# Where the weights of narrow matmuls stand in SBUF: 192 bytes into their buffers, other tiles at equal addresses

## The chip, the cores and the metric

The kernel runs on one core of one Trainium2 chip. The metric is the device time of one execution in microseconds (us). A time "of the runs" is the median of timed executions; a profile is one more execution, with its own time.

## The reference

Two layers of a diffusion backbone over 256 context tokens and 256 latent tokens of 1024 features, in float32. A layer is half a SwiGLU FFN, a token mixer (layer 0: bidirectional mLSTM; layer 1: bidirectional retention), and half an FFN; each of these six sub-layers is normed and modulated by a linear map of the condition. The last FFN runs for the latent tokens alone.

```python
def half_ffn(h, mod, g, w13, w2, j):
    return h + FFN_RES * mod[:, :, 3 * j + 2] * swiglu(modnorm(h, g, mod, j), w13, w2)
def swiglu(h, w13, w2):
    a, b = jnp.split(h @ w13, 2, axis=-1)
    return (jax.nn.silu(a) * b) @ w2
for i in range(DEPTH):
    ...
    x = half_ffn(x, mod_x, norm_g[i, 0], ffn_w13[i, 0], ffn_w2[i, 0], 0)
    ctx = half_ffn(ctx, mod_c, norm_g[i, 0], ffn_w13[i, 0], ffn_w2[i, 0], 0)
    ...
return rmsnorm(x, final_g)
```

D_MODEL is 1024, D_FF 2816.

## The kernel before

**Units.** All weights come as units of 1 MB (some of 512 KB), one DMA each from SP's queue, three units ahead, into one of three `raw` buffers. `split(n, half)` turns each half of a unit (128x1024 numbers) into a high part `wh` (ACT, L147) and a low part `wl` (DVE, L148), each in one of four buffers. TensorE (PE) then makes three products of a tile pair for each 128x128 block of weights: `mm3` (L151 to L153) multiplies high by high, high by low and low by high into the same PSUM bank. Activations are split in the same way: `xh`, `xl` (the normed stream, 512 tokens wide: 256 context, 256 latent), `gh`, `gl` (the middle of an FFN), `yh`, `yl` (the middle of retention), and `qh`, `kh`, `vh`, `Ph` with their low parts.

**Widths.** A product's moving operand has 512 columns where both segments go together, and 256 where one goes alone. The four FFNs are named by layer and place: FFN(0,0), FFN(0,1), FFN(1,0), FFN(1,1). In the first three the w2 products are 240 matmuls of 512 columns in the first of two parts, and 192 of 512 and 192 of 256 in the second: the last two units of the second part run segment by segment, so that the norm of the context segment can be made under the products of the latent one. FFN(1,1) has 22 w13 units and 11 w2 units of 48 matmuls each, all of 256 columns. Of 256 columns are also: the first two w13 units of FFN(0,1) and FFN(1,0) (192 matmuls each), the mLSTM's `qk(0)` (96) and its last two output units (192), retention's `proj_k(0)` (96), its four `proj_q` (192), its scores (96) and its eight output units with `yh`, `yl` (384).

**Addresses.** PE loads the weights of the next matmul (LDWEIGHTS) while the moving operand of the present one streams. Both are read from SBUF. In the built program `xh`, `xl`, `wh` and `wl` all start 224 bytes past a multiple of 256, and every block in them starts a multiple of 512 bytes further on. So moving and stationary operands of these products stand at **equal addresses**, as this document calls it: their distance is a multiple of 256 bytes. For `gh` and `gl` the kernel takes `shift` numbers of a filler tile `gf` ahead of them, so they stand 0 bytes (FFN(0,0)), 32 (FFN(0,1)), 64 (FFN(1,0)) and 128 (FFN(1,1)) past the weights' place. `yh` and `yl` come to stand 96 past it; retention's own products (scores, values) have equal addresses. Both ways of standing, which operand is moving and which stationary, occur: `Y<-xh,wh` may have `xh` as the stationary one.

**Order.** A scheduler orders the instructions of each engine; the first stage's order is written out by hand. The first DMAs on SP's queue are `VT` (all vectors), then `XT` (the stream); POOL's queue brings `ident` and `cst` (the two triangular masks `up` and `low`, used at L643 and L644 in the mLSTM's gates).

Of the kernel before, what the change touches and what calls it, by code (L numbers as in the profile page):

```python
# [87 lines left out]
def build(nc, tc, dr, out):  # L88
# [32 lines left out]

    V.memset(fill.tile([128, 24], F32, name="fill"), 0.0)
    ident = const.tile([128, 128], F32, name="ident")
    nc.gpsimd.dma_start(out=ident, in_=dr["c1"][:, 0:128])
    cst = const.tile([128, 258], F32, name="cst")
    nc.gpsimd.dma_start(out=cst, in_=dr["c1"][:, 128:386])
    up, low = cst[:, 0:128], cst[:, 128:256]
# [4 lines left out]
    VT = const.tile([128, 256], F32, name="VT")  # L132
    XT = const.tile([128, KT, NT], F32, name="XT")
# [7 lines left out]
    FG = VT[:, 64:72]  # L141
    CW = VT[:, 72:112]
    MB = VT[:, 112:256]

# [130 lines left out]
    def ffn(l, which, segs, groups, on_tile, on_seg, first="seg"):  # L275
# [3 lines left out]
        st = ExitStack()  # L279
        shift = (0, 8, 16, 32)[2 * l + which]  # L280
        P = {}
# [5 lines left out]
        def start(W):  # L287
            if groups:
                mp["r"] = pool("mr", 3, st)
                if first == "k":  # L290
                    mp["c"], mp["j"] = U["mc"], U["mj"]
                else:
                    mp["c"] = mc = pool("mc", 1, st).tile([128, 2, DM], F32, name="mc")
                    mp["j"] = pool("mj", 1, st).tile([128, DM], mybir.dt.bfloat16, name="mj")
                    nc.gpsimd.dma_start(out=mc.rearrange("p w k -> p (w k)"), in_=dr["cc"].to_broadcast([128, 2 * DM]))
                    for w in range(2):
                        S.activation(out=mc[:, w], in_=mc[:, w], func=AF.Silu)
            if shift:
                G.memset(pool("gf", 1, st).tile([128, shift], F32, name="gf"), 0.0)
            P["g"] = pool("g", 12, st)  # L300
            P["s"] = pool("s", 4, st)
# [3 lines left out]
        for d0, nd in parts:  # L305
            for p in range(d0, d0 + nd, 2):
                sv = {}
                for ab in range(2):
# [41 lines left out]
                    if first == "k" and p == 0:  # L350
                        def fn0(W, ab=ab, sv=sv):
                            sv["ps", ab] = U["ps", ab] = {m: bankA() for m in range(2)}
                            first_products[ab](W)
                        res.append((fn0, src, "own"))
                        late.append((lambda W, done=done: done(), None, None))
                        if ab:
                            res += [(start, None, None)] + late
                    else:
                        res.append((fn, src, "k"))
            ku = [(k, min(4, d0 + nd - k)) for k in range(d0, d0 + nd, 4)]  # L360
            fin = d0 == parts[-1][0]
            for mg in range(2):
                Y = {}
                for k0, nk in ku:
# [100 lines left out]
    def mlstm(on_tile, on_seg):  # L465
# [26 lines left out]
        def qk(u):  # L492
            src = win[:, u * 256:(u + 1) * 256].rearrange("(k p) c -> p k c", p=128)

            def fn(W):
# [10 lines left out]
                for m in range(2):  # L506
# [11 lines left out]
                    S.activation(out=X["q" if c < 4 else "k"][:, c % 4, :], in_=cv, func=AF.Silu)  # L518
            return (fn, src, "k")

# [35 lines left out]
        def wout(hh, u):  # L556
# [30 lines left out]
            def fn1(W):  # L587
# [7 lines left out]
                on_seg(1)  # L595
            return ((fn, src, "k") if hh == 0 else (fn0, src, "k") if u == 0 else (fn1, src, "k2"))

# [22 lines left out]
    def gates(X):  # L620
# [21 lines left out]
        ps = gb[:, 128:256]  # L642
        TE.matmul(ps[:, 0:32], up, lf[:, 0:32], start=True, stop=True)  # L643
        TE.matmul(ps[:, 32:64], low, lf[:, 32:64], start=True, stop=True)  # L644
        TE.matmul(ps[0:1, 64:128], ones[:, 0:1], lf, start=True, stop=True)
# [196 lines left out]
    def retention(on_tile, on_seg):  # L842
# [5 lines left out]
        def start(W):  # L848
# [6 lines left out]
            X["cos"], X["sin"] = tb[:, 1536:1792], tb[:, 1792:2048]  # L855
            dec = p.tile([128, 8], F32, name="dec")
            nc.sync.dma_start(out=dec, in_=dr["r_dec"].to_broadcast([128, 8]))
            lg = p.tile([128, 8], F32, name="lg")
            logsig(lg, dec, 8)
            nl = p.tile([128, 8], F32, name="nl")  # L860
            V.tensor_scalar(out=nl[:, 0:4], in0=lg[:, 0:4], scalar1=-128.0, scalar2=None, op0=ALU.mult)
# [21 lines left out]
        def proj_k(h):  # L883
            X[h] = H = {}

            def fn(W):
# [13 lines left out]
                rope([z[:, :, 256:512] for z in H["k"]], pp[0][:, 256:512], pp[1][:, 256:512])  # L900
            return (fn, win[:, 1024 + h * 256:1024 + (h + 1) * 256].rearrange("(k p) c -> p k c", p=128), "eo")

        def proj_q(h):
            H = X[h]

            def fn(W):
                H["q"] = pair("q", [128, 2, 256])
                pp = [bankA() for _ in range(2)]
                for hf in range(2):
                    for e in range(2):  # L910
                        for k in range(hf * 4, hf * 4 + 4):
                            mm3(pp[e][:, 0:256], [W(i, k)[:, e, :] for i in range(2)],
                                (xh[:, k, 256:512], xl[:, k, 256:512]), k == 0, k == KT - 1)
# [3 lines left out]
            return (fn, win[:, h * 256:(h + 1) * 256].rearrange("(k p) c -> p k c", p=128), "eo")  # L917

# [107 lines left out]
        def outp(h):  # L1026
            r = []
            for u in range(2):
                src = dr["r_out"][h * 512:(h + 1) * 512, u * 512:(u + 1) * 512].rearrange("(k p) c -> p k c", p=128)

                def fn(W, u=u):
# [13 lines left out]
                    if h == 3 and u == 1:  # L1045
                        on_seg(1)
                r.append((fn, src, "k"))
            return r
# [73 lines left out]
    def first_stage():  # L1122
# [144 lines left out]
    def split(n, half):  # L1267
# [8 lines left out]
        if mode == "eo":  # L1276
            src_ = src_.rearrange("p (a c e) -> p a e c", a=na, e=2)
# [32 lines left out]
    for i, (fn, src, mode) in enumerate(steps):  # L1310
# [11 lines left out]
        with ExitStack() as late:  # L1322
            if n == 2:
                for z in ("hi", "lo"):
                    late.enter_context(tc.issue_after(U[z, 5].ins))
            split_to(2 * n + (2 if mode == "k2" else 3))
        fn(Unit(n, src))
# [1 line left out]
```

## Time and profile before

| | us |
|---|---|
| median of 3 runs (1915.36 to 1919.32) | 1918.21 |
| profiled execution, its own time | 1913.94 |
| its span, first to last instruction | 1912.1 |

The span is what the rows further down divide up. PE is busy in nearly all of it; its clock was granted at 0.991 of full speed on average.

### The profile page before, as it was taken

What the parts mean: (1) busy time and instruction counts of PE and PEld (TensorE: products, weight loads), DVE (VectorE), ACT (ScalarE), POOL (GpSimd) and SP (SyncE); (2) the same over time, 40 slices, a digit from 0 to 9 for tenths busy, and PEclk for the clock granted to TensorE, in tenths of its full rate; (3) what the DMA queues carried; (4) which work ended last, traced back from release to release, by engine and by line L of the source; (5) the groups of instructions that cost most, each with busy time, mean ns of one, the idle gap of its engine ahead of it and who ended that gap; (6) DMA issues with size and microseconds to landing.
All of it is one profiled execution on the core that took longest, in us unless ns stands there. A gap on an engine that the chain in (4) does not pass through costs nothing.

```text
span 1912.1 us, 25440 instructions
## 1 busy us (share of the span) xinstructions
PE 1878.6 (98%) x10142; PEld 1617.0 (85%) x10142; DVE 1192.0 (62%) x1965; ACT 696.8 (36%) x1061; POOL 167.2 (9%) x207
## 2 busy tenths in 40 slices
PE   8999999999999999999999999999999999999998
PEld 6888888887777898888888988888898888889998
DVE  6858878566866566677764655555466555565554
ACT  4432232243553352222333422223244444444443
POOL 3000000110132210000001000000112120110001
PEclk9999999999998999999999999999999999989999
DMA  8536656223323234455542344554334244235652
GB/s 315 194 125 209 209 176 206 91 86 99 102 94 100 100 100 139 148 198 176 187 176 89 111 145 167 187 195 165 116 105 129 98 138 132 99 123 170 205 177 89
DMA packets 171689, 280.58 MB, mean 147 GB/s; under 512 B 6210, under 2 KB 108738, under 8 KB 171186
## 3 DMA queue, kind: packets, MB, share of 16 engines
q1 hardware_dynamic: 168656, 268.59, 42.0%
q0 software_dynamic: 2912, 10.36, 1.7%
q8 instruction: 80, 1.31, 0.3%
q14 instruction: 39, 0.31, 0.0%
q10 hardware_dynamic: 2, 0.01, 0.0%
HBM read 277.82 MB, written 1.11 MB: 146 GB/s over the span
## 4 chain that ended last, share of the span: by engine, by line
PE 91%; DVE 4%; ACT 2%; DMA 1%; issue 1%; POOL 1%; SPq 0%; POOLq 0%; DVEq 0%; ACTq 0%
PE A L152 18%; PE A L151 18%; PE A L153 18%; PE Y L152 11%; PE Y L151 11%; PE Y L153 11%; PE A L794 1%; PE A L797 1%; PE Y L1095 1%; DVE wl L148 1%; DMA XT<-xt 0%; DMA t<-nwd 0%; ACT wh L147 0%; DVE XT L210 0%; DVE so L551 0%
## 5 line engine op out<-in xcount | busy, mean ns | idle before, releaser
L148 DVE TENSOR_TENSOR wl<-raw,wh 128x1024 fp32r<-128x1024 f32 x360 | 448.0, 1245 | 465.9 <-ACT wh L147 465.6
L147 ACT ACTIVATE wh<-raw 128x1024 fp32r<-128x1024 f32 x360 | 382.2, 1062 | 808.1 <-PE A L152 324.7
L152 PE MATMUL A<-xl,wh 128*128 128x512 f32 (+1 forms) x1712 | 599.5, 352 | 6.8 <-DVE xl L148 6.1
L153 PE MATMUL A<-xh,wl 128*128 128x512 f32 (+1 forms) x1712 | 598.2, 351 | 0.0
L151 PE MATMUL A<-xh,wh 128*128 128x512 f32 (+1 forms) x1712 | 592.4, 352 | 5.6 <-ACT xh L1112 2.6
L152 PEld LDWEIGHTS A<-xl,wh 128*128 128x128 f32 x1712 | 325.8, 190 | 51.0 <-DVE xl L148 7.6
L151 PEld LDWEIGHTS A<-xh,wh 128*128 128x128 f32 x1712 | 321.5, 191 | 48.9 <-ACT xh L1112 2.9
L153 PEld LDWEIGHTS A<-xh,wl 128*128 128x128 f32 x1712 | 325.8, 190 | 42.4
L247 DVE CUSTOM_DVE_ANT_0 mj<-mr,mc,VT 128x1024 bf16<-128x1024 f32 x224 | 287.0, 1281 | 4.7 <-DMA mr<-mod_t 1.9
L153 PE MATMUL Y<-gh,wl 128*128 128x512 f32 (+1 forms) x704 | 246.0, 350 | 0.0
L151 PE MATMUL Y<-gh,wh 128*128 128x512 f32 (+1 forms) x704 | 245.5, 350 | 0.0
L152 PE MATMUL Y<-gl,wh 128*128 128x512 f32 (+1 forms) x704 | 245.3, 349 | 0.0
L153 PEld LDWEIGHTS Y<-gh,wl 128*128 128x128 f32 x704 | 132.3, 188 | 18.5
L152 PEld LDWEIGHTS Y<-gl,wh 128*128 128x128 f32 x704 | 132.4, 188 | 18.2
L151 PEld LDWEIGHTS Y<-gh,wh 128*128 128x128 f32 x704 | 132.3, 188 | 17.5
L152 PE MATMUL Y<-wl,xh 128*128 128x512 f32 x320 | 126.2, 395 | 0.0
L151 PE MATMUL Y<-wh,xh 128*128 128x512 f32 x320 | 125.3, 393 | 0.0
L153 PE MATMUL Y<-wh,xl 128*128 128x512 f32 x320 | 125.0, 392 | 0.0
L173 POOL TENSOR_TENSOR nacc<-nacc,nsq 128x256 f32<-128x256 f32 x50 | 41.6, 840 | 644.8 <-ACT nsq L169 643.4
L147 ACT ACTIVATE gh<-s 128x512 fp32r<-128x512 f32 (+1 forms) x88 | 48.7, 568 | 84.9 <-DVE s L338 84.9
L210 DVE SCALAR_TENSOR_TENSOR XT<-Y,GT,XT 128x256 f32<-128x256 f32 x148 | 63.8, 477 | 21.3 <-PE Y L153 21.1
L338 DVE TENSOR_TENSOR s<-s,A 128x512 f32<-128x512 f32 (+1 forms) x88 | 54.3, 619 | 28.5 <-PE A L153 28.2
(269 smaller groups left out, 1826.2 us busy)
## 6 DMA issues: line engine op xcount, KB each, us to landing
raw<-w SPq DMA_DIRECT2D x126, 1024.0 KB, 5.2
mr<-mod_t SPq DMA_DIRECT2D x128, 512.0 KB, 3.9
raw<-r_in SPq DMA_DIRECT2D x24, 1024.0 KB, 5.2
raw<-m_in SPq DMA_DIRECT2D x12, 1024.0 KB, 5.3
raw<-r_out SPq DMA_DIRECT2D x8, 1024.0 KB, 5.6
raw<-w SPq DMA_DIRECT2D x12, 512.0 KB, 3.7
w<-mod_t SPq DMA_DIRECT2D x8, 512.0 KB, 10.7
w<-mod_s SPq DMA_DIRECT2D x8, 512.0 KB, 10.6
```

The lines of the kernel that those rows point to most:

```text
L147: S.activation(out=hi, in_=src, func=AF.Copy)
L148: return V.tensor_tensor(out=lo, in0=src, in1=hi.bitcast(F32), op=ALU.subtract)
L151: TE.matmul(ps, l[0], r[0], start=first, stop=False)
L152: TE.matmul(ps, l[0], r[1], start=False, stop=False)
L153: return TE.matmul(ps, l[1], r[0], start=False, stop=last)
L173: G.tensor_tensor(out=N[s][0], in0=N[s][0], in1=sq, op=ALU.add)
L210: V.scalar_tensor_tensor(out=XT[:, k, seg(s)], in0=ps, scalar=gate[:, s, k:k + 1], in1=XT[:, k, seg(s)], op0=ALU.mult, op1=ALU.add)
L247: V.tensor_tensor_reduce(out=mp["j"], in0=raw[i], in1=mp["c"][:, w], scale=1.0, scalar=MB[:, l * 72 + f:l * 72 + f + 1], op0=ALU.mult, op1 ...
L338: V.tensor_tensor(out=g[:, a:z], in0=sv[m][:, a:z], in1=ps[m][:, a:z], op=ALU.mult)
L794: TE.matmul(ps[:, i, :], E[:, i * 4 + g * 2 + c], v[:, s * 2 + c, 2 * i + g, :], start=True, stop=(n == 0))
L797: TE.matmul(ps[:, i, :], WI[o:o + 64, i, c * 128:c * 128 + 128], X["C", d, n - 1][o:o + 64, i], start=False, stop=True)
L1095: TE.matmul(ps, U["w", k][:, 0, c * 128:(c + 1) * 128], SC.rearrange("p (w k) -> p k w", w=2)[:, c], start=(c == 0), stop=(c == KT - 1))
```

## The change

Four things. **(1)** `wh` and `wl` become 64 numbers (256 bytes) longer, and a unit whose matmuls are 256 columns wide, marked by an `n` at the end of its mode, is written 48 numbers (192 bytes) into them. A unit with 512 columns starts at 0 as before. **(2)** The filler `gf` goes, so `gh` and `gl` stand at equal addresses with a buffer's start in all FFNs; a small `fill0` brings all these tiles to a multiple of 256 bytes. `yh` and `yl` get there too. Retention's `q` pair is placed 64 bytes into a longer tile. In the built program every product of 256 columns with weights, and every score, then has its moving operand 64 bytes past the stationary one (counted modulo 256, that is 192 before it), and every product of 512 columns with weights has equal addresses (but for the mLSTM's gate weights `b4`, 96 before and after). **(3)** `VT` is cut in two: 72 columns stay for good (288 bytes a partition), 184 (`VB`: conv weights and modulation biases, 736 bytes) go to a pool that is closed ahead of retention. **(4)** The masks leave `cst` and are loaded at the mLSTM's start into a buffer of tag `hs`; retention's small decay tiles share one tile.

```diff
@@ ffn
-        shift = (0, 8, 16, 32)[2 * l + which]
+        narrow = "n" if len(segs) == 1 else ""
...
-            if shift:
-                G.memset(pool("gf", 1, st).tile([128, shift], F32, name="gf"), 0.0)
...
-                        res.append((fn, src, "k"))
+                        res.append((fn, src, "kn" if p == 0 and first == "seg" else "k" + narrow))
...
-                        res.append((fn1, src, "k2") if last else (fn0, src, "k"))
+                        res.append((fn1, src, "k2n") if last else (fn0, src, "kn"))
                     else:
-                        res.append((fn, src, "k"))
+                        res.append((fn, src, "k" + narrow))
@@ mlstm, retention
+            cst = X["p2"].tile([128, 2, 4, 128], F32, name="hs", tag="hs")[:, 0, :2]
+            nc.gpsimd.dma_start(out=cst.rearrange("p a t -> p (a t)"), in_=dr["c1"][:, 128:384])
...
-                H["q"] = pair("q", [128, 2, 256])
+                H["q"] = [z[:, 16:528].rearrange("p (e t) -> p e t", e=2) for z in pair("q", [128, 576])]
@@ first_stage
         nc.sync.dma_start(out=VT, in_=dr["vec"])
+        nc.sync.dma_start(out=VB, in_=dr["veb"])
@@ split
-        hi = wsp.tile([128, 1024], F32R, name="wh", tag="wh")[:, :na * b]
-        lo = wsp.tile([128, 1024], F32R, name="wl", tag="wl")[:, :na * b]
+        o = 48 if mode[-1] == "n" and mode != "own" else 0
+        hi = wsp.tile([128, 1088], F32R, name="wh", tag="wh")[:, o:o + na * b]
+        lo = wsp.tile([128, 1088], F32R, name="wl", tag="wl")[:, o:o + na * b]
```

PE and ACT have the same instructions in the same order before and after. DVE has one memset more at the start (`fill0`). POOL loses three memsets of `gf`, and its DMA of the masks moves. First POOL's queue from the start, before:

```order
6 L124 DMA ident<-c 128x128
7 L126 DMA cst<-c 128x258
8 L160 ISA
9 L160 TENSOR_TENSOR rsb<-rsa,mhalf 128x4
...
15 L1180 TENSOR_TENSOR x_227<-XT,bc 128x512
16 L486 MEMSET b_3041 128x1024
17 L487 MEMSET b_3042 128x1024
18 L173 TENSOR_TENSOR nacc<-nacc,nsq 128x256 x8
```

And the same stretch of POOL's queue after, up to the first squares (`nacc`) of the norm behind FFN(0,0):

```order
6 L126 DMA ident<-c 128x128
7 L161 ISA
8 L161 TENSOR_TENSOR rsb<-rsa,mhalf 128x4
...
14 L1183 TENSOR_TENSOR x_232<-XT,bc 128x512
15 L475 DMA hs<-c 128x256
16 L488 MEMSET b_3048 128x1024
17 L489 MEMSET b_3049 128x1024
18 L174 TENSOR_TENSOR nacc<-nacc,nsq 128x256 x8
```

The mask DMA has gone from the first microseconds to the place ahead of the two memsets that prepare the mLSTM. SP's queue, which starts the kernel's main loads, begins so before:

```order
1 L1131 DMA VT<-vec 128x256
2 L1133 DMA XT<-xt 128x1024 x4
3 L1081 DMA w<-mod_t 128x1024
4 L1082 DMA w<-mod_s 128x1024
5 L1088 DMA raw<-w 128x4x256
```

And so after:

```order
1 L1133 DMA VT<-vec 128x72
2 L1134 DMA VB<-veb 128x184
3 L1136 DMA XT<-xt 128x1024 x4
4 L1083 DMA w<-mod_t 128x1024
5 L1084 DMA w<-mod_s 128x1024
```

One DMA more stands ahead of the four that bring `XT`.

## Rows read from the trace of the kernel before

**Rows 1.** The page: busy time by engine, and the chain that ended last.

```profile
PE 1878.6 (98%) x10142; PEld 1617.0 (85%) x10142; DVE 1192.0 (62%) x1965; ACT 696.8 (36%) x1061; POOL 167.2 (9%) x207
...
PE 91%; DVE 4%; ACT 2%; DMA 1%; issue 1%; POOL 1%; SPq 0%; POOLq 0%; DVEq 0%; ACTq 0%
```

**Rows 2.** Waits of PE: for whom; us, times, longest.

```profile
PE A L152 <- DVE xl L148: 6.1, 6, 1.7
PE Y L1162 <- DVE acc L1157: 4.1, 1, 4.1
```

**Rows 3.** Stretches: us, busy (x) of PE, PEld, DVE, ACT, POOL; clock, DMA, GB/s.

```profile
152.89:207.29 54.40, 54.40 (x241) 45.05 (x240) 48.46 (x75) 11.17 (x12) 0.00 (x0) 1.00 0.67 222
792.52:848.52 56.00, 56.00 (x241) 44.98 (x240) 43.63 (x66) 11.18 (x12) 0.00 (x0) 1.00 0.58 192
1161.84:1216.79 54.95, 54.95 (x241) 45.07 (x240) 31.70 (x46) 11.16 (x12) 0.00 (x0) 1.00 0.57 201
```

**Rows 4.** Stretches as in rows 3, with 256 columns.

```profile
382.47:396.02 13.55, 13.55 (x114) 13.54 (x113) 4.03 (x7) 2.86 (x6) 1.48 (x2) 1.00 0.25 79
1024.98:1038.17 13.19, 13.19 (x114) 13.19 (x113) 4.02 (x7) 2.85 (x6) 1.48 (x2) 1.00 0.26 81
1392.43:1405.74 13.31, 13.31 (x114) 13.30 (x113) 4.02 (x7) 2.86 (x6) 1.48 (x2) 1.00 0.24 79
1769.54:1798.02 28.48, 28.48 (x242) 28.48 (x241) 15.63 (x20) 11.23 (x12) 0.00 (x0) 1.00 0.61 206
1798.02:1867.13 69.11, 69.11 (x578) 69.11 (x577) 37.73 (x48) 32.45 (x46) 0.00 (x0) 1.00 0.56 183
1521.07:1526.72 5.65, 5.65 (x48) 5.64 (x47) 3.93 (x6) 2.60 (x3) 0.00 (x0) 1.00 0.25 70
```

**Rows 5.** Two neighbouring stretches of 512 columns in the mLSTM: qkv weights, gate weights.

```profile
425.31:428.03 2.72, 2.72 (x13) 2.25 (x12) 2.72 (x5) 0.61 (x2) 0.00 (x0) 1.00 0.00 0
428.27:433.17 4.90, 4.90 (x22) 3.94 (x21) 3.95 (x6) 1.27 (x2) 0.52 (x1) 1.00 0.67 212
```

**Rows 6.** Weight loads of the w2 products in 152.9:207.2; ns least, median, most.

```profile
L153 PEld LDWEIGHTS Y<-gh,wl x80: 187/188/188, 153.1 to 206.8; 128*128 128x128 f32 x80
```

**Rows 7.** The splits: L147 by form, then L148 (least, median, most ns).

```profile
L147 ACT ACTIVATE wh<-raw 128x1024 fp32r<-128x1024 f32 x360 | 382.2, 1062 | 808.1 <-PE A L152 324.7 <-PE Y L152 242.3 <-issue 171.0
...
L148 DVE TENSOR_TENSOR wl<-raw,wh x360: 1207/1226/2242, 21.8 to 1892.7; 128x1024 fp32r<-128x1024 f32 x180
```

**Rows 8.** Waits of PE in the stretches 395:430, then 1412:1440.

```profile
PE A L152 <- DVE xl L148: 2.4, 3, 1.7
...
PE A L152 <- DVE xl L148: 1.6, 1, 1.6
```

**Rows 9.** The start: issues on SP's queue; then DMAs in 0:30, KB and us to landing.

```profile
0.74 0.38 SPq L1131 DMA_DIRECT2D VT<-vec  x1
1.18 2.31 SPq L1133 DMA_DIRECT2D XT<-xt  x4
...
DMA packets 4545, 10.50 MB, mean 350 GB/s; under 512 B 351, under 2 KB 2527, under 8 KB 4544
XT<-xt SPq DMA_DIRECT2D x4, 512.0 KB, 6.9
cst<-c POOLq DMA_DIRECT2D x1, 129.0 KB, 5.6
```

**Rows 10.** POOL in 346:373, in order of time; then the masks' first reader.

```profile
347.23 0.95 POOL L486 MEMSET b<- 128x1024 f32 x1 [312.13 <-DVE GP L221]
369.06 2.14 POOL L173 TENSOR_TENSOR nacc<-nacc,nsq 128x256 f32<-128x256 f32 x3 [19.98 <-ACT nsq L169]
...
L643 PE MATMUL A<-lf,cst x2: 192/234/275, 450.8 to 450.8; 128*128 128x32 f32 x2
```

**Rows 11.** The two stretches past the start in which PE's clock was at half.

```profile
595.50:612.60 17.10, 16.08 (x53) 12.24 (x52) 5.45 (x26) 4.19 (x17) 1.50 (x3) 0.50 0.24 82
1704.90:1715.10 10.20, 8.05 (x37) 7.67 (x37) 6.91 (x18) 5.42 (x12) 0.71 (x1) 0.50 0.31 103
```

More of the change, by code (lines that the diff above doesn't have):

```diff
@@ L60 @@
             A["c_ctx"].reshape(8, 128), A["c"].reshape(8, 128), A["norm_g"].reshape(48, 128),
-            A["final_g"].reshape(8, 128), A["m_conv_w"].reshape(40, 128), A["mod_b"].reshape(144, 128)], 0).T,
+            A["final_g"].reshape(8, 128)], 0).T,
+        "veb": np.concatenate([A["m_conv_w"].reshape(40, 128), A["mod_b"].reshape(144, 128)], 0).T,
         "cc": np.concatenate([A["c_ctx"].reshape(1, 1024), A["c"].reshape(1, 1024)], 1),
@@ L122, in build @@
     V.memset(fill.tile([128, 24], F32, name="fill"), 0.0)
+    V.memset(const.tile([128, 8], F32, name="fill0"), 0.0)
     ident = const.tile([128, 128], F32, name="ident")
     nc.gpsimd.dma_start(out=ident, in_=dr["c1"][:, 0:128])
-    cst = const.tile([128, 258], F32, name="cst")
-    nc.gpsimd.dma_start(out=cst, in_=dr["c1"][:, 128:386])
-    up, low = cst[:, 0:128], cst[:, 128:256]
     ones = const.tile([128, 128], F32, name="ones")
@@ L131, in build @@
     V.memset(mhalf, -0.5)
-    VT = const.tile([128, 256], F32, name="VT")
+    VT = const.tile([128, 72], F32, name="VT")
+    sv = ExitStack()
+    VB = pool("vb", 1, sv, side="right").tile([128, 184], F32, name="VB")
     XT = const.tile([128, KT, NT], F32, name="XT")
@@ L141, in build @@
     FG = VT[:, 64:72]
-    CW = VT[:, 72:112]
-    MB = VT[:, 112:256]
+    CW = VB[:, 0:40]
+    MB = VB[:, 40:184]
     def split2(src, hi, lo):
@@ L474, in start @@
             X["dr"] = pool("mxd", 1, st, space=bass.MemoryType.DRAM)
+            cst = X["p2"].tile([128, 2, 4, 128], F32, name="hs", tag="hs")[:, 0, :2]
+            nc.gpsimd.dma_start(out=cst.rearrange("p a t -> p (a t)"), in_=dr["c1"][:, 128:384])
+            X["up"], X["low"] = cst[:, 0], cst[:, 1]
             wg = t2k(n=256).rearrange("p (k c) -> p k c", k=KT)
@@ L518, in fn @@
                     S.activation(out=X["q" if c < 4 else "k"][:, c % 4, :], in_=cv, func=AF.Silu)
-            return (fn, src, "k")
+            return (fn, src, "kn" if u == 0 else "k")
         def vo(u):
@@ L595, in fn1 @@
                 on_seg(1)
-            return ((fn, src, "k") if hh == 0 else (fn0, src, "k") if u == 0 else (fn1, src, "k2"))
+            return ((fn, src, "k") if hh == 0 else (fn0, src, "kn") if u == 0 else (fn1, src, "k2n"))
         def part(f, *a):
@@ L642, in gates @@
         ps = gb[:, 128:256]
-        TE.matmul(ps[:, 0:32], up, lf[:, 0:32], start=True, stop=True)
-        TE.matmul(ps[:, 32:64], low, lf[:, 32:64], start=True, stop=True)
+        TE.matmul(ps[:, 0:32], X["up"], lf[:, 0:32], start=True, stop=True)
+        TE.matmul(ps[:, 32:64], X["low"], lf[:, 32:64], start=True, stop=True)
         TE.matmul(ps[0:1, 64:128], ones[:, 0:1], lf, start=True, stop=True)
@@ L855, in start @@
             X["cos"], X["sin"] = tb[:, 1536:1792], tb[:, 1792:2048]
-            dec = p.tile([128, 8], F32, name="dec")
+            z = p.tile([128, 64], F32, name="lg")
+            dec, lg, nl = z[:, 0:8], z[:, 16:24], z[:, 32:40]
             nc.sync.dma_start(out=dec, in_=dr["r_dec"].to_broadcast([128, 8]))
-            lg = p.tile([128, 8], F32, name="lg")
             logsig(lg, dec, 8)
-            nl = p.tile([128, 8], F32, name="nl")
             V.tensor_scalar(out=nl[:, 0:4], in0=lg[:, 0:4], scalar1=-128.0, scalar2=None, op0=ALU.mult)
@@ L900, in fn @@
                 rope([z[:, :, 256:512] for z in H["k"]], pp[0][:, 256:512], pp[1][:, 256:512])
-            return (fn, win[:, 1024 + h * 256:1024 + (h + 1) * 256].rearrange("(k p) c -> p k c", p=128), "eo")
+            return (fn, win[:, 1024 + h * 256:1024 + (h + 1) * 256].rearrange("(k p) c -> p k c", p=128),
+                    "eo" if h else "eon")
         def proj_q(h):
@@ L916, in fn @@
                 rope(H["q"], pp[0][:, 0:256], pp[1][:, 0:256])
-            return (fn, win[:, h * 256:(h + 1) * 256].rearrange("(k p) c -> p k c", p=128), "eo")
+            return (fn, win[:, h * 256:(h + 1) * 256].rearrange("(k p) c -> p k c", p=128), "eon")
         def proj_vg(h, vg):
@@ L1046, in fn @@
                         on_seg(1)
-                r.append((fn, src, "k"))
+                r.append((fn, src, "kn"))
             return r
@@ L1250, in build @@
     steps += ffn(1, 0, both, [(1, range(4, 6)), (1, range(10, 18))], *into(N4, 1, 1))
+    steps.append((lambda W: sv.close(), None, None))
     steps += retention(*into(N5, 1, 2))
@@ L1272, in split @@
         na = min(a - half * (1024 // b), 1024 // b)
[L1273 to L1274 removed]
+        o = 48 if mode[-1] == "n" and mode != "own" else 0
+        hi = wsp.tile([128, 1088], F32R, name="wh", tag="wh")[:, o:o + na * b]
+        lo = wsp.tile([128, 1088], F32R, name="wl", tag="wl")[:, o:o + na * b]
         src_ = raw[n][:, half * 1024:half * 1024 + na * b]
[L1276 removed]
+        if mode[:2] == "eo":
             src_ = src_.rearrange("p (a c e) -> p a e c", a=na, e=2)
@@ L1325, in build @@
                     late.enter_context(tc.issue_after(U[z, 5].ins))
-            split_to(2 * n + (2 if mode == "k2" else 3))
+            split_to(2 * n + (2 if mode[:2] == "k2" else 3))
         fn(Unit(n, src))
```

## The prediction

> **What bounds the kernel now.** The page comes first: PE is busy in 98% of the span, DVE in 62%, and 91% of the chain that ended last is PE's [rows 1]. The list of waits says how little of the rest is waiting: PE's largest sum for one cause is 6.1 us, of 1912.1 [rows 2]. So time is saved where PE's matmuls follow each other faster, and nearly nowhere else. A matmul's own duration doesn't tell this, since its end is modelled and overlaps the next. What does is a stretch that holds nothing but matmuls of one kind: its length over the number of weight loads in it (the count under PE includes a matmul already under way at the left edge).
>
> Three such stretches hold the same work, the 240 matmuls of the first part of w2, in the three FFNs of two segments; only the place of the moving operand differs [rows 3]. At equal addresses they take 54.40 us, 226.7 ns each. 32 bytes apart they take 56.00 us (233.3), 64 bytes apart 54.95 us (229.0). PE is busy throughout all three, at full clock.
>
> At 256 columns the sign turns round [rows 4]. The first three stretches are 113 matmuls of the last w2 units of the same three FFNs: 13.55 us at equal addresses (119.9 ns), 13.19 at 32 bytes (116.7), 13.31 at 64 (117.8). The next two are FFN(1,1): w2, 128 bytes apart, 240 matmuls in 28.48 us (118.7 ns); w13, equal addresses, 576 matmuls (12 units of 48) in 69.11 us (120.0 ns). The last is retention's output, 96 bytes apart: 47 in 5.65 us (120.2 ns).
>
> That it is the distance between the two operands, and not where the moving one stands, is seen in the mLSTM [rows 5]. There `xh` stands as ever, but the gate weights stand 96 bytes off: 21 matmuls take 4.90 us (233.3 ns), right behind 12 in 2.72 us (226.7 ns) with ordinary weights.
>
> The Trainium skill has a rule that speaks against this change ("TensorE: Matmul & The Clock Gate", Part 2, the step on LDWEIGHTS): PE has two independent read ports in SBUF, one for the moving operand and one for weight loads, and loading the next weights takes no bandwidth from the running matmul. By it the distance of the two would be without effect, and the change worth nothing. The trace disagrees: stretches alike in all but this distance differ by up to 6.6 ns a matmul.
>
> Each weight load lasts 187 to 188 ns [rows 6]; that is less than a 512-column matmul's 226.7 and more than a 256-column one's 120, so loads fall differently on the streams of the two widths. Why one width likes equal addresses and the other not, I can't read from rows; I use the measured spacing.
>
> **The change, part by part.**
>
> *FFN middles back to equal addresses, 512 columns.* Per FFN of two segments 240 + 192 = 432 matmuls. FFN(0,1) goes from 233.3 to 226.7: 432 x 6.67 = 2.9 us saved. FFN(1,0) goes from 229.0 to 226.7: 432 x 2.29 = 1.0 us. FFN(0,0) stays. Sum 3.9 us.
>
> *256 columns, all to 64 bytes apart, 117.8 ns.* From 120.0: FFN(1,1)'s w13, 22 x 48 = 1056; the first w13 units of FFN(0,1) and FFN(1,0), 384; `qk(0)` 96; the mLSTM's output 192; `proj_k(0)` 96; `proj_q` 192: 2016 x 2.2 = 4.4 us. The w2 tail of FFN(0,0), 192 x 2.1 = 0.4 us. That of FFN(0,1) loses, since 32 bytes was better: 192 x 1.1 = 0.2 us lost. That of FFN(1,0) stays. FFN(1,1)'s w2, from 118.7: 528 x 0.9 = 0.5 us. Retention's output, from 120.2: 384 x 2.4 = 0.9 us. Its scores, which have no long stretch of their own, taken as w13: 96 x 2.2 = 0.2 us. Sum 6.2 us.
>
> The row for 64 bytes is one with `gh` moving and was made by shifting the moving operand forward; now the weights are shifted by 192, which gives the same distance modulo 256. That 256 is a period the rows support in part: equal addresses were counted modulo 256 in all stretches. Bounds for the 2016: nothing, if the period were longer and this place no better than 0; and 2016 x 3.3 = 6.6 us, if it were as good as 32 bytes (116.7). I take the row at 64, as the nearest.
>
> *What of it is not on the path.* Behind an FFN's tail PE waits for the next norm, 2.4 us in one such place, 1.6 in another [rows 8]; what PE gains in the second half of a tail, or in the units paced by the norm, is waited away. I count `qk(0)`, half of FFN(0,0)'s tail, and about 100 matmuls of other first units as lost: (96 + 96 + 100) x 2.2 = 0.6 us. Some 37 matmuls run at half clock [rows 11]; 0.1 us at most.
>
> *The splits.* ACT needs 1062 ns and DVE mostly 1226 ns for a half unit [rows 7]; narrow ones now read one place and write another, 192 bytes on. Below: no gain, as PE doesn't wait for them. Above: the slowest row of the same line, 2242 ns. In FFN(1,1) a unit has 69.11 / 12 = 5.76 us, of which DVE is busy 37.73 / 12 = 3.14 [rows 4]; two splits at 2242 would add 2.0 and still fit. So 0 either way; the cover is gone only from about 1226 + 1300 = 2.5 us a split.
>
> *The start.* SP issues one DMA more ahead of `XT`; the first issues are 0.44 us apart (0.74 to 1.18). On the other side the 129 KB of `cst` no longer share the engines with `XT`: at 350 GB/s that is 0.37 us [rows 9]. Bounds: 0.4 us lost (the issue counts, the bytes don't) to 0.4 us gained. I take 0. The memset `fill0` on DVE lies before anything has landed.
>
> *The masks.* Their DMA is now issued by POOL at about 347 us, ahead of two memsets; POOL has 20 us of nothing behind these until `nacc` at 369, and the masks are read at 450.8 [rows 10]. Issue and landing (5.6 us for `cst`, [rows 9]) are covered; were the cover gone, they would cost those 6 us. The memsets and the `nacc` behind them are what queues behind a late mask buffer; from about 20 us late on the norm would wait. The three `gf` memsets are idle POOL time: nothing. `VB` is needed by the modulation sums, which are done long before retention takes its place, so its release is nobody's wait.
>
> **Sum.** 3.9 + 6.2 - 0.6 - 0.1 = 9.4 us saved. Against the profiled execution's own 1913.94 that gives 1904.5. The runs' median lies 4.3 us above it, at 1918.21; I predict for the runs: 1908.8, say 1909, which is 0.49% less.
>
> **Rivals.**
>
> *The weights' side gains nothing.* What was measured for 256 columns was measured with the moving operand shifted; `xh` with shifted weights could stay at 120.0. Then the 2016 and the scores gain nothing, and retention's output, whose moving operand and weights both change place, only what I counted: 9.4 - 4.6 + 0.4 (of the lost 0.6) = 5.2 us, 1913. For it: no stretch shows shifted weights at 256 columns. Against: the gate weights show at 512 that moving the weights counts as much as moving the other [rows 5].
>
> *No effect of distance.* The stretches of rows 3 and 4 could differ by something else about these FFNs, and the distance itself be without effect; then nothing is saved and nothing lost: 1918. For it: each FFN has its own distance, so no stretch shows two. Against: the three stretches hold the same instructions, and the ordinary and the gate weights in one phase differ too [rows 5]. This is the time that the Trainium skill's rule of the two ports would give.
>
> *The gain goes into half-clock time.* The two stretches at half clock hold 16.08 and 8.05 us of busy PE and 1.0 and 2.2 us of idle PE [rows 11]. Half clock doubles the work's time, so a third such stretch would cost 4 to 8 us, and one less gives as much. For it: where PE waits for others, a faster PE waits longer. Against: no wait grows by more than some tenths. Time: 1914 to 1917.
>
> *Slower.* It is where the moving operand itself stands that counts. After the change all of `xh`, `xl`, `gh`, `gl` stand 0 bytes past a multiple of 256, which is where `gh` stood in FFN(0,1), the stretch at 233.3 ns. Then every 512-column matmul of the three FFNs (3 x 432 and some 2976 of w13) would go at 233.3: 2976 + 432 more at +6.6, 432 at +4.4, about 24 us lost, and narrow ones at 116.7 give back 2500 x 3.2 = 8 us. Time: 1918 + 24 - 8 = 1934. It decides from half that effect. For it: place and distance change together in rows 3. Against: rows 5, where `xh` keeps its place and slows, with only 21 matmuls; retention's output isn't at its best at 96.
>
> **How the numbers follow.** Chances: the forecast 0.70, weights' side 0.12, no effect 0.04, half clock 0.08, slower 0.06. A change can be told from none here from about 0.2%, 3.8 us. The forecast's own range is 1906 to 1912: the sum's bounds (start 0.4 each way; the 2016 between 3 and 6.6 us) and the 1 to 3 us by which runs lie off their median. Weights' side ends at 1913, inside "faster" but near its edge; I share it 0.08 to 0.04. Of the half-clock case 0.02 would still be faster, and 0.01 of the whole slower. So faster 0.80, same 0.13, slower 0.07. The range of 8 in 10 takes in that rival and the lower edge of the half-clock one, reaches below the forecast's own by a half-clock stretch that grows shorter, and leaves out the rest: 1904.5 to 1915.
>
> **What would show it.** In the stretches after: w2's 240 matmuls at 54.4 us in all three FFNs; FFN(1,1)'s 576 of w13 in 67.8 us instead of 69.11; its 240 of w2 in 28.3; the tail of FFN(0,1) slightly longer, 13.3 us instead of 13.19. `wl` still at 1226 ns. PE's waits within a microsecond of now, the first matmul of L1162 at the same time within 0.4 us. Wrong it would be if the 576 stay at 69.1 (weights' side), if x and g stretches at 512 columns go to 56 per 240 (place), if a third stretch at half clock appears, or if PE starts to wait for `wl`.

## The result, and the profile after

The median of five runs is 1901.71 us (1894.75 to 1907.25), that of five runs of the kernel before beside them 1918.21 (1914.24 to 1919.32). The ratio is 0.9936, interval [0.9915, 0.9956]; the quotient of the two medians alone would be 0.9914. Five runs of a kernel spread by up to 12.5 us, so neither figure is the size of the change to the last us. Run again later, the changed kernel gave 0.9944 [0.9922, 0.9965]. The profiled execution took 1906.76 us, its span 1904.7, at a mean clock of 0.989.

The page, busy time by engine and the chain, as in [rows 1]:

```profile
PE 1872.2 (98%) x10142; PEld 1613.4 (85%) x10142; DVE 1192.3 (63%) x1966; ACT 696.2 (37%) x1061; POOL 165.8 (9%) x204
...
PE 91%; DVE 5%; ACT 2%; issue 1%; DMA 1%; POOL 0%; DVEq 0%; POOLq 0%; SPq 0%; ACTq 0%
```

PE's busy time fell by 6.4 us for the same 10142 instructions; it is still the bound. Now the three 512-column stretches of [rows 3], in the view of stretches:

```profile
153.29:207.69 54.40, 54.40 (x241) 45.05 (x240) 48.47 (x75) 11.16 (x12) 0.00 (x0) 1.00 0.66 223
796.10:850.50 54.40, 54.40 (x241) 45.05 (x240) 43.35 (x66) 11.16 (x12) 0.00 (x0) 1.00 0.59 196
1162.25:1216.65 54.40, 54.40 (x241) 45.05 (x240) 31.70 (x46) 11.16 (x12) 0.00 (x0) 1.00 0.58 203
```

All three hold their 240 matmuls in 54.40 us. The 256-column stretches of [rows 4], in the same order and view:

```profile
382.84:396.15 13.31, 13.31 (x115) 13.31 (x113) 4.03 (x7) 2.87 (x6) 1.48 (x2) 1.00 0.24 80
1025.63:1038.94 13.31, 13.31 (x114) 13.29 (x113) 4.03 (x7) 2.87 (x6) 1.49 (x2) 1.00 0.24 80
1391.77:1405.08 13.31, 13.31 (x114) 13.28 (x113) 4.03 (x7) 2.86 (x6) 1.47 (x2) 1.00 0.23 79
1763.98:1792.25 28.27, 28.27 (x242) 28.27 (x241) 15.62 (x19) 11.22 (x12) 0.00 (x0) 1.00 0.63 209
1792.25:1860.09 67.84, 67.84 (x578) 67.84 (x577) 37.75 (x48) 32.44 (x46) 0.00 (x0) 1.00 0.56 185
1519.90:1525.43 5.53, 5.53 (x48) 5.53 (x47) 3.88 (x6) 2.61 (x3) 0.00 (x0) 1.00 0.22 69
```

Every one is at 117.8 ns a matmul: 13.31/113, 28.27/240, 67.84/576 and 5.53/47. One place is faster. Retention's last three output units, behind their first matmul, take 16.10 us for 143 weight loads, in the kernel before 17.04. By the starts of the matmuls that is 113.3 ns each, 120.0 before. First the kernel before, then after:

```profile
1685.46:1702.50 17.04, 17.04 (x144) 17.04 (x143) 12.66 (x19) 7.86 (x12) 3.96 (x5) 1.00 0.44 137
1683.30:1699.40 16.10, 16.10 (x144) 16.10 (x143) 12.54 (x19) 7.54 (x12) 3.56 (x4) 1.00 0.45 139
```

The weight loads are what they were in [rows 6], here those of FFN(0,1), and so are the splits of [rows 7]:

```profile
L154 PEld LDWEIGHTS Y<-gh,wl x80: 187/188/188, 796.3 to 850.1; 128*128 128x128 f32 x80
```

```profile
L148 ACT ACTIVATE wh<-raw 128x1024 fp32r<-128x1024 f32 x360 | 382.2, 1062 | 801.9 <-PE A L153 321.1 <-PE Y L153 243.3 <-issue 169.4
```

```profile
L149 DVE TENSOR_TENSOR wl<-raw,wh x360: 1207/1226/2237, 20.6 to 1885.5; 128x1024 fp32r<-128x1024 f32 x180
```

PE's waits, as in [rows 2]: the same 6.1 us for `xl`, and 3.2 instead of 4.1 for the first norm (L1165, L1162 before).

```profile
PE A L153 <- DVE xl L149: 6.1, 6, 1.7
PE A L796 <- DVE b L784: 3.4, 2, 2.4
PE Y L1165 <- DVE acc L1160: 3.2, 1, 3.2
```

The start, as in [rows 9]: SP's first issues, then the DMA of `XT` (median landing 5.4 us, 6.9 before). `XT` is issued 0.45 us later and lands earlier.

```profile
0.73 0.38 SPq L1133 DMA_DIRECT2D VT<-vec  x1
1.16 0.42 SPq L1134 DMA_DIRECT2D VB<-veb  x1
1.63 1.87 SPq L1136 DMA_DIRECT2D XT<-xt  x4
```

```profile
XT<-xt SPq DMA_DIRECT2D x4, 512.0 KB, 5.4
```

POOL's queue where the masks went, and their reader, as in [rows 10]:

```profile
348.08 0.63 POOL L475 DMA_DIRECT2D hs<-c  x1 [314.12 <-DVE GP L222]
348.71 0.97 POOL L488 MEMSET b<- 128x1024 f32 x1
...
369.46 2.13 POOL L174 TENSOR_TENSOR nacc<-nacc,nsq 128x256 f32<-128x256 f32 x3 [18.89 <-ACT nsq L170]
```

```profile
L645 PE MATMUL A<-lf,hs x2: 192/234/275, 450.7 to 450.7; 128*128 128x32 f32 x2
```

POOL issues the load in 0.63 us and still waits 18.89 before `nacc`; nothing waits for the masks. Last, the stretches at half clock as in [rows 11], of which there are now three:

```profile
50.16:53.57 3.41, 3.32 (x8) 2.64 (x9) 2.80 (x7) 1.64 (x4) 0.00 (x0) 0.50 0.44 154
596.29:623.60 27.31, 26.75 (x84) 20.36 (x84) 11.95 (x53) 11.12 (x37) 5.66 (x6) 0.50 0.15 52
1702.21:1709.04 6.83, 4.67 (x21) 4.30 (x21) 4.58 (x14) 3.61 (x9) 0.71 (x1) 0.50 0.46 154
```

The one at 50 us is new, the next 10 us longer than before, the last 3 us shorter. By the starts of the same matmul in both traces, this execution is 1.9 us ahead of the old one at 50 us and 0.4 behind at 55; it is level with it at 577 us and 4.3 us behind at 628. So it gave back 2.3 and 4.4 us at these two places, and gained nearly everywhere else. A third stretch at half clock is one of the signs of being wrong that the prediction named; it appeared, though short. That is the open point of the result: the matmuls gained what was worked out, but what an execution spends at half clock moves by as much.

### The profile page after: what moved, and what is told of

Read it like the earlier page. It is cut to its first block, busy times and chain, and to the rows that moved or that the text cites. A ratio compares the mean times of both kernels' runs of the same rounds, so it can differ in the third digit from the quotient of the medians.

```text
span 1904.7 us, 25437 instructions
## 1 busy us (share of the span) xinstructions
PE 1872.2 (98%) x10142; PEld 1613.4 (85%) x10142; DVE 1192.3 (63%) x1966; ACT 696.2 (37%) x1061; POOL 165.8 (9%) x204
## 4 chain that ended last, share of the span: by engine, by line
PE 91%; DVE 5%; ACT 2%; issue 1%; DMA 1%; POOL 0%; DVEq 0%; POOLq 0%; SPq 0%; ACTq 0%
PE A L153 18%; PE A L154 18%; PE A L152 17%; PE Y L153 11%; PE Y L152 11%; PE Y L154 11%; PE A L796 1%; PE A L799 1%; DVE wl L149 1%; PE Y L1097 1%; ACT wh L148 0%; DVE XT L211 0%; PE A L763 0%; DVE t L201 0%; DVE mj L1101 0%
## 5 line engine op out<-in xcount | busy, mean ns | idle before, releaser
L148 ACT ACTIVATE wh<-raw 128x1024 fp32r<-128x1024 f32 x360 | 382.2, 1062 | 801.9 <-PE A L153 321.1
L248 DVE CUSTOM_DVE_ANT_0 mj<-mr,mc,VB 128x1024 bf16<-128x1024 f32 x224 | 286.8, 1281 | 3.7 <-DMA mr<-mod_t 0.9
L148 ACT ACTIVATE gh<-s 128x512 fp32r<-128x512 f32 (+1 forms) x88 | 48.7, 568 | 84.0 <-DVE s L337 84.0
```

The costliest lines, as they stand in the source:

```text
L148: S.activation(out=hi, in_=src, func=AF.Copy)
L248: V.tensor_tensor_reduce(out=mp["j"], in0=raw[i], in1=mp["c"][:, w], scale=1.0, scalar=MB[:, l * 72 + f:l * 72 + f + 1], op0=ALU.mult, op1 ...
```

## The experiments

Ratios are to the kernel before, run on the same chip beside the experiment.

**One part each: the weights at 0.** The changed kernel, narrow weights at the start of their buffers:

```diff
-        o = 48 if mode[-1] == "n" and mode != "own" else 0
+        o = 0
```

> The changed kernel, but narrow weights are written at the start of their buffers, so that nearly all products of 256 columns stand at equal addresses. All addresses of tiles are those of the changed kernel. Distance theory: 576 matmuls of FFN(1,1)'s w13 take 69.1 us again (119.9 ns) and its 240 of w2 28.8 us; some 3470 narrow matmuls lose 2.1 ns each, so about 7 us more than the changed kernel, leaving 3.8 us of the matmul gain against the kernel before, plus the start's 1 to 2 us: ratio to before about 0.997. Place theory (it matters where the moving operand stands, not the distance): 117.8 ns stays in all of them, and so does the ratio, 0.994. Half-clock theory (what the changed kernel gained beyond 9.4 us is luck in stretches at half clock): the granted clocks of the runs scatter as those of the kernel before, and a run's time goes by its clock.

Measured: 1909.44 us, ratio 0.9985 [0.9973, 0.9997]. FFN(0,1)'s w2, then FFN(1,1)'s w13:

```profile
791.28:845.68 54.40, 54.40 (x241) 45.05 (x240) 43.33 (x66) 11.18 (x12) 0.00 (x0) 1.00 0.60 196
1792.72:1861.84 69.12, 69.12 (x579) 69.12 (x577) 37.69 (x48) 32.49 (x46) 0.00 (x0) 1.00 0.55 183
```

512 columns keep their 54.40, 256 columns are back at 120.0, so the place theory falls. The expected ratio of 0.997 lies outside the interval. My sum had forgotten that without `gf` the tails and FFN(1,1)'s w2 also fall back to 120: 3.9 - 0.6 - 0.4 - 0.7 = 2.2 us, a ratio of 0.9988.

**One part each: the middles shifted.** The changed kernel with `shift` and `gf` as before:

```diff
+        shift = (0, 8, 16, 32)[2 * l + which]
...
+            if shift:
+                G.memset(pool("gf", 1, st).tile([128, shift], F32, name="gf"), 0.0)
```

> The changed kernel, but with the filler ahead of the FFN middles again (0, 32, 64, 128 bytes); the narrow weights stay 192 bytes into their buffers. Distance theory: w2's 240 matmuls go back to 56.0 us in FFN(0,1) and 54.95 us in FFN(1,0), 3.8 us more in all than the changed kernel for 864 matmuls of 512 columns; w13 of FFN(1,1) stays at 67.8 us; the narrow tails now stand 64, 96, 128 bytes apart and FFN(1,1)'s w2 192, of which 128 was 118.7 ns and 192 is not known. Ratio to before about 0.996. Place theory: with the narrow gain owed to the place of xh, all of it stays as well; it does not tell the two apart at 256 columns, but at 512 it expects 233 ns wherever a moving operand stands 32 or 64 past, whatever the weights do, which is the same here.

Measured: 1905.99 us, ratio 0.9962 [0.9947, 0.9977], some 7.3 us. FFN(0,1)'s w2 and FFN(1,1)'s w2:

```profile
796.35:852.35 56.00, 56.00 (x241) 44.99 (x240) 43.62 (x66) 11.17 (x12) 0.00 (x0) 1.00 0.57 192
1767.68:1794.89 27.21, 27.21 (x243) 27.21 (x241) 15.53 (x19) 11.24 (x12) 0.00 (x0) 1.00 0.63 212
```

FFN(0,1) is back at 233.3 ns. FFN(1,1)'s middles stand 128 bytes on and its weights 192, so their distance is 192, and there a matmul takes 113.4 ns, less than any stretch had shown. With that, 9.4 - 3.9 + 528 x 4.4 ns - 0.6 (two tails at 96 and 128) = 7.2 us.

**The masks at the start again.** The kernel with weights at 0, and the old buffers and mask load:

```diff
+    cst0 = const.tile([128, 256], F32, name="cst")
+    nc.gpsimd.dma_start(out=cst0, in_=dr["c1"][:, 128:384])
```

> The kernel of the run before last (narrow weights at 0), with buffers back to their old length and the two masks loaded in the first microseconds from POOL's queue, as before the change; the split of the vectors stays. If the masks' DMA is what held up the stream at the start, the first matmul on the norm's sums starts again near 13.9 us (12.8 in the changed kernel) and the four loads of the stream take about 6.9 us to land instead of 5.4. If it was the smaller first DMA of vectors, the start stays at 12.8 us. The time after the start is that of the kernel with narrow weights at 0.

One run: 1909.14 us; the kernel with the weights at 0 alone had a median of 1909.44. PE's first norm matmul starts at 13.5 us; in the profiles with the masks at the start it came at 12.7, 13.5 and 13.9, in ten with the masks moved at 12.6 to 13.9. The masks' place can't be seen in the start.

**Every distance, in steps of 32 and of 16 bytes.** Each unit `n` gets its own place:

```diff
-        o = 48 if mode[-1] == "n" and mode != "own" else 0
+        o = n % 8 * 8 if mode != "own" else 0
```

> The changed kernel, but unit number n is written (n mod 8) x 32 bytes into its buffers, whatever its width, so that every distance from 0 to 224 in steps of 32 bytes occurs at both widths with ordinary weights. Distance theory: 512 columns: 226.7 ns at 0, 233.3 at 32, 229.0 at 64, about 233 at 96; 256 columns: 119.9 at 0, 116.7 at 32, 117.8 at 64, 118.7 at 128; w13 and w2 units at the same distance agree within 1 ns. Place theory: all units of a width alike. The other distances are not known; one of them may be better than those used.

> The changed kernel, but unit n is written (n mod 16) x 16 bytes into its buffers, so that distances of 16, 48, 80 and so on occur too. If the spacing goes by whole steps of 6.67 ns (16 of PE's cycles at 2.4 GHz) averaged over the three products of a block, as the sweep in steps of 32 bytes reads (113.3, 115.6, 117.8, 120.0; 226.7, 228.9, 233.3), all new distances fall on such values: 106.7 plus 2.22 times a whole number at 256 columns. No theory here says which; a distance that holds 113.3 ns in all units would be worth 4.4 ns x 3470 = 15 us.

One run each: 1932.62 and 1931.09 us. (The second has `n % 16 * 4`.) The mean ns from one matmul's start to the next, by distance (moving less stationary, modulo 256), both kernels together, `x` or `g` moving:

| bytes | 512 columns | 256 columns | bytes | 512 columns | 256 columns |
|---|---|---|---|---|---|
| 0 | 226.7 | 119.9 | 128 | 232.4 to 233.3 | 118.5 to 120.0 |
| 16 | 226.7 to 228.5 | 119.7 to 120.0 | 144 | 233.3 | 119.8 |
| 32 | 233.3 | 116.7 to 117.8 | 160 | 234.2 | 117.3 to 120.0 |
| 48 | 231.9 to 233.3 | 116.7 | 176 | 231.8 | 118.8 |
| 64 | 228.9 | 117.8 or 113.4 | 192 | 233.3 | 117.8 or 113.3 |
| 80 | 229.9 | 118.1 to 118.3 | 208 | 233.3 | 117.8 |
| 96 | 233.3 | 119.7 to 120.0 | 224 | 233.3 | 118.3 |
| 112 | 233.4 | 118.3 to 119.8 | 240 | 226.7, once 233.3 | 118.3 |

Equal addresses are the best place for 512 columns and among the worst for 256. The steps that were expected of the finer sweep fall: 116.7 and 118.3 are not among them. Nor is distance all that counts. Where the weights are the moving operand, 240 bytes give 236.0 ns at 512 columns (second sweep, at 1529 and 1671 us) in place of 226.7. And at several distances 256 columns have more than one pace, furthest apart at 64 and 192. Four units of 256 columns in the kernel with steps of 16 bytes, at 64, 64, 192 and 208:

```profile
1765.35:1771.01 5.66, 5.66 (x51) 5.66 (x49) 3.61 (x6) 3.12 (x5) 0.00 (x0) 1.00 0.54 171
1850.44:1855.88 5.44, 5.44 (x51) 5.44 (x49) 3.60 (x6) 3.12 (x5) 0.00 (x0) 1.00 0.55 180
1808.58:1813.34 4.76, 4.76 (x45) 4.76 (x43) 2.96 (x3) 2.13 (x2) 0.00 (x0) 1.00 0.72 246
1889.94:1895.59 5.65, 5.65 (x50) 5.65 (x49) 2.45 (x2) 2.12 (x2) 0.00 (x0) 1.00 0.57 182
```

The first two are 48 matmuls at the same distance and differ by 0.22 us; the third is 42 in 4.76 (113.3 ns), the last 48 in 5.65 (117.7).

**The changed kernel again.**

> The changed kernel once more, on the chip and beside the kernel before as the others, since the first five runs scattered by 12.5 us. Distance theory: its gain is the sum of the matmul terms, 9.4 us, and up to 1 us at the start: ratio about 0.9945, median near 1903 where the kernel before has 1913. Half-clock theory: runs with a mean granted clock of 0.986 to 0.988 are some 7 us slower than those at 0.992 and 0.993, in both kernels, and at equal clock the difference is the same 9 to 11 us. If the first measurement was the true size, the ratio is 0.9936 again, 12 us.

Measured: 1906.17 us (1900.97 to 1908.21, 6 runs), before 1915.39, ratio 0.9944 [0.9922, 0.9965]. Runs nearly sort by their mean clock: at 0.988 the changed kernel takes 1907.6 and 1908.2, the old one 1917.3 to 1919.9; at 0.993 1901.0 against 1910.6. At equal clock they are some 10 us apart; each alone spreads over 7 to 10.

**Fillers against the half clock.** PE waits 2.4 us for `b` ahead of the stretch at half clock (in the changed kernel, below), and several times for up to 1.1 us ahead of the second, in the norm behind retention. Five matmuls that nobody reads are put into these waits:

```diff
+    def warm(n):
+        ps = bankY()
+        for _ in range(n):
+            TE.matmul(ps, ones, XT[:, 0, :], start=True, stop=True)
...
+        if (l, j) == (1, 2):
+            warm(2)
...
+        if (s, hh) == (0, 1):
+            warm(3)
```

> The changed kernel with five matmuls more, whose results nobody reads: three of 512 columns in float32 (0.85 us each at full clock) behind the scores ahead of the stretch at half clock in the mLSTM, where PE waits 2.8 us for DVE, and two in the wait for the norm behind retention. Half-clock theory: PE has no longer idle time ahead of the fall, the stretch of 17 or 27 us near 596 us goes or shortens, the runs lie closer together, mean clock 0.995, and the median falls by 3 to 6 us against the changed kernel although work is added. Rival: the clock falls for the small matmuls that follow and not for the idle time; then the stretch stays and the run is as before or up to 2 us longer by the fillers.

Measured: 1897.15 us (1896.31 to 1902.63), ratio 0.9910 [0.9891, 0.9929], mean clock 0.996 or 0.997 in five of six runs. That is 9.0 us below the changed kernel beside it, where 3 to 6 were expected. Run a second time, beside the next experiment:

> The changed kernel with fillers once more, on the same chip as the two others of this call, so that the differences to them are taken at the same time: 1897 within 1.5 us, ratio 0.9895 to 0.992.

Measured: 1894.88 us (1894.77 to 1897.08, 5 runs), ratio 0.9903 [0.9884, 0.9922]: the ratio as expected, the time 0.6 us below the range that was expected. PE in order of time, in the changed kernel:

```profile
590.23 1.71 PE L763 MATMUL A<-q,k 64*128 64x128 f32 x16
594.35 0.68 PE L796 MATMUL A<-v,b 128*128 128x129 f32 x4 [2.41 <-DVE b L784]
```

And with the fillers (a float32 matmul has two records), then that kernel's stretch from 597 us in the view of stretches:

```profile
590.84 2.84 PE L215 MATMUL Y<-XT,ones 128*128 128x512 f32 x6
593.52 0.61 PE L806 MATMUL A<-v,b 128*128 128x129 f32 x4
```

```profile
597.20:621.10 23.90, 23.11 (x118) 18.02 (x117) 17.38 (x59) 11.74 (x34) 7.55 (x7) 1.00 0.13 45
```

The idle 2.41 us are filled, and the clock stays at 1.00 where it was 0.50. At the second place, near 1700 us, all five profiles with fillers still have 3.4 to 6.8 us at half clock, against 3.4 to 10.2 in the eight without; what the two matmuls there are worth isn't shown.

**The kernel before, with the same fillers.** This takes the half clock out of both sides.

> The kernel before with the same five unread matmuls behind the scores of intra(0,1) and between norm_rstd and norm_bcast of the norm behind retention; nothing else changed. The gain of the placement alone is then what lies between this kernel and the changed one with fillers. Theory (the terms of the sum are right in size, and the rest of what the runs scatter is half-clock time): the long stretches at half clock near 596 and 1705 us go, runs scatter by less than 4 us, and the median is 1897.2 + 9.4 = 1906.6, between 1905 and 1908.5. Rival 1 (the placement itself gives more, 12 us or over, through something that the sum lacks): 1909 or above. Rival 2 (the placement gives less, and half-clock time gave the rest): 1903 or below. Rival 3 (the fillers act only in the changed kernel): above 1912, with the stretches still there.

Measured: 1907.59 us, ratio 0.9976 [0.9958, 0.9994]. Its 12 runs lie in two groups: eight at a clock of 0.996 or 0.997, 1906.0 to 1908.0, and four at 0.990, 1915.8 to 1917.8; the profiled one is of the second:

```profile
597.84:621.73 23.89, 23.33 (x73) 17.81 (x72) 11.08 (x48) 9.48 (x32) 6.12 (x6) 0.50 0.12 45
```

So here the fillers keep the clock up in two executions of three, and a stretch of 24 us at half clock costs some 10 us. The expected spread of less than 4 us was missed: it is 11.8. The median of the eight is 1906.4, that of the ten runs of the changed kernel with fillers at 0.995 or above 1896.6: 9.9 us less. The second five of them, which alone ran on the same chip, give 11.5. Part by part, by the starts of the same matmul in the two profiles with fillers (before, and the changed kernel's second):

| from, in the kernel before | us saved | in it | by the sum |
|---|---|---|---|
| 360 to 561 | 0.52 | tail of FFN(0,0), `qk(0)` | 0.2 (0.6, less 0.4 waited away) |
| 561 to 641 | 10.86 | the stretch at half clock | |
| 641 to 721 | 0.75 | mLSTM output, first units of FFN(0,1) | 0.8 |
| 721 to 1042 | 2.80 | FFN(0,1) | 2.7 |
| 1042 to 1403 | 1.43 | FFN(1,0) | 1.4 |
| 1403 to 1684 | 1.53 | retention, but for its last three output units | 1.4 |
| 1684 to 1724 | 1.77 | half clock 6.83 against 3.41 us: 1.1; retention's last three output units: 0.9, of which 0.3 waited away | 0.3 |
| 1724 to the end | 2.65 | FFN(1,1) | 2.8 |

Without the two places at half clock that is 9.7 us, and with retention's last units some 10.4. By these parts the rivals that gave the placement 12 us or more, or far less, fall; by the times alone, 9.9 or 11.5 us, 12 is not far off. That the fillers act in the changed kernel alone falls too.

**Distance 192.** The changed kernel with fillers; narrow weights stand 64 bytes into their buffers, every fourth unit 48, so the distances are 192 and 208:

```diff
-        o = 48 if mode[-1] == "n" and mode != "own" else 0
+        o = (16 if n % 4 else 12) if mode[-1] == "n" and mode != "own" else 0
```

> The changed kernel with fillers, but narrow weights are written 64 bytes into their buffers instead of 192 (every fourth unit 48 bytes), so the moving operand of the narrow products stands 192 bytes past the stationary one, or 208. In the sweep of 16 bytes every unit at 192 that came behind one at 208 ran at 113.3 ns a matmul, not 117.8. Theory (the place behind the 208 decides): 2562 matmuls at 192 times 4.45 ns is 11.4 us less, some 0.5 us of it waited away, so 1886. Rival 1 (the 113.3 holds only while nothing interrupts, and is lost with the first wait or LDWEIGHTS of another kind until the next unit at 208): between 1889 and 1894, with units in which the spacing turns from 113.3 to 117.8 part way. Rival 2 (the 113.3 was chance, the spacing at 192 is 117.8): 1897.

Measured: 1890.01 us (1888.61 to 1891.62), ratio 0.9875 [0.9856, 0.9894]. Three units of FFN(1,1) at 192, and the one at 208 behind them:

```profile
1735.79:1752.11 16.32, 16.32 (x146) 16.32 (x145) 8.92 (x11) 7.91 (x11) 0.00 (x0) 1.00 0.48 155
1752.11:1757.76 5.65, 5.65 (x50) 5.65 (x49) 3.73 (x6) 2.73 (x4) 0.00 (x0) 1.00 0.61 204
```

144 matmuls in 16.32 us are 113.3 ns, and all units at 192 in FFN(1,1) run so. Between 640 and 1700 us it is as the first rival had it: in a unit from 665.8 us the spacing is 113.3 until one matmul comes 201 ns behind the last, and 117.8 from there on. The time is in that rival's range. Is the unit at 208 what brings it? All narrow units at 192:

```diff
-        o = (16 if n % 4 else 12) if mode[-1] == "n" and mode != "own" else 0
+        o = 16 if mode[-1] == "n" and mode != "own" else 0
```

> As the kernel with the narrow weights 64 bytes into their buffers, but without the units at 48 bytes: every narrow unit has its moving operand 192 bytes past the stationary one, none 208. Theory (the pace at 192 hangs on what ran before: only a unit at 208 brings it to 113.3 ns, and without one it stays at 117.8): FFN(1,1)'s w13 stretches at 117.8 ns a matmul, time as with the fillers alone, 1895 to 1897. Rival (192 is simply the better place, and finds 113.3 ns by itself as long as nothing interrupts): FFN(1,1) at 113.3 throughout, the quarter of its 1584 matmuls that ran at 208 gains 396 x 4.45 ns = 1.8 us, so 1888.

Measured: 1888.21 us (1885.56 to 1889.88), ratio 0.9865 [0.9841, 0.9888], the fastest kernel here. FFN(1,1)'s w2 and w13:

```profile
1747.62:1774.82 27.20, 27.20 (x242) 27.20 (x241) 15.60 (x20) 11.26 (x12) 0.00 (x0) 1.00 0.64 217
1774.82:1840.10 65.28, 65.28 (x578) 65.28 (x577) 37.74 (x48) 32.51 (x46) 0.00 (x0) 1.00 0.59 193
```

576 in 65.28 and 240 in 27.20 us: 113.3 ns throughout, with no unit at 208. The theory falls, the rival holds. It is the spacing that decides this, since the times of the two kernels overlap. Most of the tails and `proj_q` stay at 117.8 at the same distance, so what sets the pace on entry stays open.

## Why the prediction was right, point by point

*512 columns, 3.9 us.* Right: 54.40 us in all three FFNs, and 56.00 as soon as the middles are shifted.

*256 columns, 6.2 us.* Right: 117.8 ns in nearly all of them, also for `xh` with shifted weights, which no row had shown. Retention's last three output units found 113.3 ns, which gave 0.6 us more than the 0.3 counted for them; nothing in the prediction led to expect this. The rival "the weights' side gains nothing" falls by 67.84 against 69.12 us. That it goes by the distance modulo 256, and not by the place of one operand, is shown twice: 192 gives 113.3 ns with the weights moved by 64, and 113.4 with middles at 128 and weights at 192. Distance doesn't set the pace alone, as the two paces at 64 and 192 show.

*No effect of distance, and the slower rival.* Both fall: the sweeps change nothing but the weights' place and move the spacing from 226.7 to 234 and from 113.3 to 120 ns. The Trainium skill's rule of two independent read ports ("TensorE: Matmul & The Clock Gate", Part 2, the step on LDWEIGHTS), taken to mean that the distance has no effect, doesn't hold for the spacing of these matmuls. By which part of the chip the two operands meet, no run shows.

*What is waited away, 0.6 us.* Somewhat too much: the tail of FFN(0,0) and `qk(0)` gave 0.52 us instead of 0.2.

*Splits, masks.* Right at nothing: 1062 and 1226 ns as before, and 18.89 us of idle POOL behind the mask load.

*The start, 0 within 0.4.* The means, 13.4 us in three profiles and 13.0 in ten, are as near as the bound says; single executions are not: the first norm matmul starts anywhere from 12.6 to 13.9 us, whatever the masks do. The 1.1 us that the profile after gained there are such a difference between executions.

*The sum, 9.4 us.* Some 10.4, added up from the places that are not at half clock; what the sum lacks is mainly retention's last units and gains behind FFN(0,0) that it counted as waited away.

*The time and the range.* As a ratio the forecast was 0.9951, which both measured intervals hold. The time, 1909 us, is 7 above the first median, which lies below the range. The step that failed is "the 1 to 3 us by which runs lie off their median", and with it the half-clock rival, to which I gave a size but no spread. One stretch at half clock, there or not, is worth 10 us; runs of the kernel before reach from 1910.3 to 1920.2 in the later comparisons, with medians of 1913.0 to 1915.4 instead of the 1918.21 that I started from. Less 9.4, these give 1903.6 to 1906, which is where the median of the changed kernel's 11 runs lies (1905.8). That the first five of them came out lower, one at 1894.75 with a mean clock no higher than that of runs at 1901, no run explains. That rival's mechanism is real: the profiled execution gave back 4.4 us by it. But the kernel before loses time in the same way: its 57 later runs and the changed kernel's 11 have the same mean clock, 0.990, so it takes little from the ratio. Whether the change itself makes the first stretch longer (27.3 us in the three profiles with narrow weights 192 bytes in and no fillers, 17.1 in the five others without fillers, the two sweeps among them) stays open.

## What to carry to other kernels

Where matmuls follow each other without gaps, read their start-to-start spacing by width and by the distance of moving and stationary address modulo 256, and place each width on its own best distance: 0 for 512 columns here, 192 for 256. And before a difference of half a per cent is read from medians, look at what each execution spent at half clock; a few matmuls that nobody reads in the idle places ahead of it were worth 9.0 us in the changed kernel, about as much as the change itself, and 5.4 in the kernel before, by the medians.

## What the runs showed of the hardware that was not expected

- At one distance there can be two paces: at 64 and at 192 bytes 256-column matmuls run at 117.8 or at 113.3 ns for whole units. Behind one matmul that came 201 ns after the last, 113.3 became 117.8; in retention's output, behind one that came 194 ns after (193 in the changed kernel), 117.8 became 113.3. In the kernel with units at 208, one that came 192 ns after changed nothing there.
- Most mean spacings fall on a few sharp values, each the same over a hundred matmuls and more: 113.3, 116.7, 117.8, 118.3, 118.8 and 120.0 ns at 256 columns, 226.7, 228.9, 229.9, 231.8, 233.3 and 234.2 at 512.
- Three float32 matmuls in an idle time of 2.41 us kept the granted clock at full (2.4 GHz) for the 24 us behind it in four profiles of five; in all eight profiles without them it was half (1.2 GHz) there for 17 to 27 us.
